# Where the rows of an elementwise multiply-and-GELU lie in DRAM: 5 KB and 64 KB rows of a partition in two stretches, or in one row of 69 KB

## The chip, the cores and the metric

The kernel runs on one core of a Trainium2 chip. The time is device microseconds (us) of that core, the median of several executions. The profile is of one execution, taken by the hardware profiler; it is told with its own span, the time from the first to the last instruction.

The core has 16 DMA engines, which move data between DRAM and the on-chip memory of 128 partitions. A transfer is issued by one instruction of a queue (here SP's and ACT's) and runs on the 16 engines as packets. VectorE (DVE) multiplies, ScalarE (ACT) computes the GELU. In this document KB is 1024 bytes, MB and GB/s are decimal as in the profile.

## What is computed

```python
# x, y: float32 of 1024 x 4096
z = x * y
out = 0.5 * z * (1 + np.tanh(np.sqrt(2 / np.pi) * (z + 0.044715 * z ** 3)))
```

Every output element depends on the elements of x and y at the same place and on nothing else. So any way of sharing the 4,194,304 elements among the 128 partitions will do, as long as x, y and out use the same one.

## The kernel before

Each partition gets 32,768 elements (128 KB) of x, y and out. They are cut into three pieces, named by their columns in the on-chip tensor `xs`: `PIECES` (line 14) has columns 0 to 1280 (5 KB of a partition), 1280 to 17664 (64 KB) and 17664 to 32768 (59 KB). x stays in `xs` whole; the product and then the GELU overwrite it in place. y goes through `ys`, which holds 20,440 elements of a partition, so the y pieces share its space (`Y_LOADS`, line 16: the columns and the place in `ys`).

`columns` (line 51) says where a piece lies in DRAM. It takes the flat tensor, picks the stretch that belongs to the piece (128 times the piece's columns, starting at 128 times its first column), and cuts this stretch into 128 rows, one for each partition. So before the change the 5 KB rows of all partitions follow each other without a gap in the first 640 KB, the 64 KB rows in the next 8 MB, and the 59 KB rows in the rest. The same function serves x, y and out.

There are nine transfers of 128 rows each, three for x, y and out. Their order:

- The 5 KB x rows (SP) and the 64 KB x rows (ACT) are issued at the very start; `_hoist` (line 25) moves the two instructions ahead of the program's opening.
- SP waits for the 5 KB x rows (line 81) and issues the 64 KB y rows, then the 59 KB x rows.
- SP issues the 59 KB y rows when three multiplications are done (their place in `ys` is then free), and the 5 KB y rows when four are (`Y_FREE`, line 18).
- VectorE multiplies the 64 KB piece in four steps of 4096 columns, the 59 KB piece in seven steps of 2048 and one of 768, and the 5 KB piece in one step (`STEPS`, line 20; line 99). ScalarE follows each step (line 107).
- SP stores in the order of `STORES` (line 21): the 64 KB rows, the 59 KB rows, the 5 KB rows. The first store waits until the 59 KB y rows have landed (line 114), and each for ScalarE (line 115).
- At the end SP waits for the stores and clears the semaphores (lines 117 to 122).

Of the kernel before, what the change touches and what calls it, by code (L numbers as in the profile page):

```python
# [1 line left out]

# [4 lines left out]


F32 = mybir.dt.float32
GELU = mybir.ActivationFunctionType.Gelu_apprx_tanh  # L10

PIECES = [(0, 1280), (1280, 17664), (17664, 32768)]

Y_LOADS = [(1280, 17664, 4056), (17664, 32768, 0), (0, 1280, 15104)]

Y_FREE = [0, 3, 4]

STEPS = [[4096] * 4, [2048] * 7 + [768], [1280]]  # L20
STORES = [(1280, 17664), (17664, 32768), (0, 1280)]
Y_BUF = 20440


def _hoist(nc, issued):

    here = nc.cur_bb.bb.instructions
    first = nc.main_func.blocks[0].instructions
    for ins in issued:
        del here[next(k for k, i in enumerate(here) if i is ins or i.name == ins.name)]  # L30
    engine = issued[0].engine
    at = next(
        k
        for k, i in enumerate(first)
        if i.engine == engine and type(i).__name__ == "InstDrain"
    )
    first[at:at] = issued


@with_exitstack  # L40
def kernel(
    ctx: ExitStack,
    tc: tile.TileContext,
    x: bass.AP,
    y: bass.AP,
    out: bass.AP,
):
    nc = tc.nc
    P = nc.NUM_PARTITIONS

    def columns(t, a, b):

        flat = t.flatten_outer_dims().rearrange("r c -> (r c)")
        pa, pb = next(q for q in PIECES if q[0] <= a and b <= q[1])
        return flat[P * pa : P * pb].rearrange("(p c) -> p c", p=P)[:, a - pa : b - pa]


    tc.close()
    tc.compile()

    xs = nc.alloc_sbuf_tensor("xs", [P, PIECES[-1][1]], F32).ap()
    ys = nc.alloc_sbuf_tensor("ys", [P, Y_BUF], F32).ap()
    sem_x = [nc.alloc_semaphore(f"sem_x{i}") for i in range(len(PIECES))]
    sem_y = [nc.alloc_semaphore(f"sem_y{i}") for i in range(len(Y_LOADS))]
    sem_mul = nc.alloc_semaphore("sem_mul")
    sem_act = nc.alloc_semaphore("sem_act")
    sem_o = [nc.alloc_semaphore(f"sem_o{i}") for i in range(len(STORES))]

    def load_x(i, engine=nc.sync):
        a, b = PIECES[i]  # L70
        return engine.dma_start(out=xs[:, a:b], in_=columns(x, a, b)).then_inc(sem_x[i], 16)

    def load_y(i):
        a, b, r = Y_LOADS[i]
        return nc.sync.dma_start(
            out=ys[:, r : r + b - a], in_=columns(y, a, b)
        ).then_inc(sem_y[i], 16)

    _hoist(nc, [load_x(0).ins])
    _hoist(nc, [load_x(1, nc.scalar).ins])  # L80
    nc.sync.wait_ge(sem_x[0], 16)
    load_y(0)
    load_x(2)
    for i in range(1, len(Y_LOADS)):
        if Y_FREE[i]:
            nc.sync.wait_ge(sem_mul, Y_FREE[i])
        load_y(i)

    nc.scalar.wait_ge(sem_x[0], 16)
    n = 0  # L90
    done = {}
    for i, (a, b, r) in enumerate(Y_LOADS):
        for j, (xa, xb) in enumerate(PIECES):
            if xa <= a < xb:
                nc.vector.wait_ge(sem_x[j], 16)
        nc.vector.wait_ge(sem_y[i], 16)  # L96
        c = a
        for w in STEPS[i]:
            nc.vector.tensor_mul(  # L99
                out=xs[:, c : c + w],  # L100
                in0=xs[:, c : c + w],
                in1=ys[:, r + c - a : r + c - a + w],
            ).then_inc(sem_mul, 1)
            n += 1
            done[c + w] = n
            nc.scalar.wait_ge(sem_mul, n)
            nc.scalar.activation(  # L107
                out=xs[:, c : c + w], in_=xs[:, c : c + w], func=GELU
            ).then_inc(sem_act, 1)
            c += w  # L110

    for i, (a, b) in enumerate(STORES):
        if i == 0:
            nc.sync.wait_ge(sem_y[-2], 16)
        nc.sync.wait_ge(sem_act, done[b])
        nc.sync.dma_start(out=columns(out, a, b), in_=xs[:, a:b]).then_inc(sem_o[i], 16)
    for i in range(len(STORES) - 1):
        nc.sync.wait_ge(sem_o[i], 16)
    nums = sorted(s.num for s in [*sem_x, *sem_y, *sem_o[:-1], sem_mul, sem_act])
    assert nums == list(range(nums[0], nums[-1] + 1))  # L120
    nc.sync.sem_clear(range(nums[0], nums[-1] + 1))
    nc.sync.wait_ge(sem_o[-1], 16).then_inc(sem_o[-1], -16)


# [1 line left out]
_INS = ['x', 'y']  # L126
_OUTS = [((1024, 4096), 'float32')]


# [23 lines left out]
```

## Time and profile before

| | |
|---|---|
| median of 3 runs | 119.72 us (119.71 to 119.9) |
| span of the profiled execution | 118.5 us |
| VectorE busy | 35.2 us in 13 instructions |
| ScalarE busy | 30.9 us in 14 instructions |
| moved by DMA | 50.33 MB: 33.55 read, 16.78 written |
| mean rate over the span | 425 GB/s |

The profiled execution's time outside its span is not in the profile; the span is 1.2 us below the median. The 50.33 MB are the two inputs and the output once each.

How the profile's DMA rows are read: each row of a transfer is one packet here. A queue's row gives the number of packets (a few tiny ones are semaphore updates), the megabytes, and the time that its packets took as a share of 16 engines' span. In a table of stretches each line has the stretch, its length, the busy time and number of instructions of VectorE, ScalarE and GpSimd, the granted TensorE clock, the DMA engines' busy share, and GB/s. A packet is counted whole where it starts, so a share can come out a little over 1 in a stretch that is cut through packets.

The transfers, from their issue to the landing of the last byte (the 64 KB ones come without their size in this view):

```profile
xs<-in_x_dram SPq DMA_DIRECT2D x1, 7552.0 KB, 46.5
ys<-in_y_dram SPq DMA_DIRECT2D x1, 7552.0 KB, 22.5
out_dram<-xs SPq DMA_DIRECT2D x1, 7552.0 KB, 20.4
xs<-in_x_dram SPq DMA_DIRECT2D x1, 640.0 KB, 13.6
ys<-in_y_dram SPq DMA_DIRECT2D x1, 640.0 KB, 19.7
out_dram<-xs SPq DMA_DIRECT2D x1, 640.0 KB, 20.8
xs<-in_x_dram ACTq DMA_DIRECT2D x1, 30.4
ys<-in_y_dram SPq DMA_DIRECT2D x1, 29.0
```

These are long because a transfer waits in its queue behind others: the 640 KB of y's 5 KB rows land 19.7 us after their issue.

### The profile page before, as it was taken

The numbers are of one execution on the slowest core, as the hardware profiler recorded it, in microseconds if no ns is written. First come the engines' busy times: TensorE is split into PE (matmuls) and PEld (weight loads), VectorE is DVE, ScalarE is ACT, GpSimd is POOL, SyncE is SP. The second block draws the span as 40 slices with busy tenths as digits, with TensorE's granted clock in tenths as the row PEclk, the third lists the DMA queues.
The fourth block names the chain that finished last, engine by engine and source line by source line (L and its number), as shares of the span: only waits on it lengthen the run. The fifth ranks groups of instructions, "written<-read, shape, count | busy, mean of one in ns | idle before, by whom it ended". The sixth has DMA issues, their size and how long they took to land.

```text
span 118.5 us, 83 instructions
## 1 busy us (share of the span) xinstructions
DVE 35.2 (30%) x13; ACT 30.9 (26%) x14; POOL 0.2 (0%) x4
## 2 busy tenths in 40 slices
DVE  0000000000000069999920000059999940000000
ACT  0000000000000000999975000006998990000000
POOL 0000000000000000000000000000000000000000
DMA  9888899889988897798797797798899887977975
GB/s 492 382 382 382 354 597 464 354 354 465 597 354 354 354 632 347 326 632 347 326 632 347 326 632 347 326 575 354 354 531 531 354 354 326 653 326 326 653 326 221
DMA packets 1296, 50.33 MB, mean 425 GB/s; under 512 B 144, under 2 KB 144, under 8 KB 528
## 3 DMA queue, kind: packets, MB, share of 16 engines
q1 hardware_dynamic: 1152, 41.94, 82.3%
q10 hardware_dynamic: 144, 8.39, 16.5%
HBM read 33.55 MB, written 16.78 MB: 425 GB/s over the span
## 4 chain that ended last, share of the span: by engine, by line
DMA 55%; DVE 24%; ACT 3%; issue 1%; DVEq 0%
DMA ys<-in_y_dram 43%; DVE xs L99 24%; DMA xs<-in_x_dram 11%; ACT xs L107 3%; DVEq L96 0%
## 5 line engine op out<-in xcount | busy, mean ns | idle before, releaser
L99 DVE TENSOR_TENSOR xs<-xs,ys 128x2048 f32<-128x2048 f32 (+3 forms) x13 | 35.2, 2778 | 60.9 <-DMA ys<-in_y_dram 60.9
L107 ACT ACTIVATE xs<-xs 128x2048 f32<-128x2048 f32 (+3 forms) x13 | 29.6, 2300 | 19.6 <-DVE xs L99 19.6
L107 ACT ACT_TABLE_LOAD x1 | 1.3, 1283 | 47.2 <-DVE xs L99 47.2
L137 POOL MEMSET const-uint8-127<- 128x1 uint8 x1 | 0.1, 102 | 0.0
L137 POOL MEMSET const-bfloat16-1.0<- 128x1 bf16 x1 | 0.1, 101 | 0.0
L137 POOL MEMSET const-float32-0.0<- 128x1 f32 x1 | 0.1, 98 | 0.2 <-issue 0.2
L137 POOL MEMSET const-float32-1.0<- 128x1 f32 x1 | 0.1, 98 | 0.0
## 6 DMA issues: line engine op xcount, KB each, us to landing
xs<-in_x_dram SPq DMA_DIRECT2D x1, 7552.0 KB, 46.5
ys<-in_y_dram SPq DMA_DIRECT2D x1, 7552.0 KB, 22.5
out_dram<-xs SPq DMA_DIRECT2D x1, 7552.0 KB, 20.4
xs<-in_x_dram SPq DMA_DIRECT2D x1, 640.0 KB, 13.6
ys<-in_y_dram SPq DMA_DIRECT2D x1, 640.0 KB, 19.7
out_dram<-xs SPq DMA_DIRECT2D x1, 640.0 KB, 20.8
xs<-in_x_dram ACTq DMA_DIRECT2D x1, 30.4
ys<-in_y_dram SPq DMA_DIRECT2D x1, 29.0
```

The source lines that it names most:

```text
L99: nc.vector.tensor_mul(out=xs[:, c : c + w], in0=xs[:, c : c + w], in1=ys[:, r + c - a : r + c - a + w],).then_inc(sem_mul, 1)
L107: nc.scalar.activation(out=xs[:, c : c + w], in_=xs[:, c : c + w], func=GELU).then_inc(sem_act, 1)
L137: nc = _bacc.Bacc("TRN2", target_bir_lowering=False, num_devices=1)
```

## The change

A second table, `STRETCHES`, has two stretches in place of the three pieces, and `columns` looks a piece up in it. The first stretch has columns 0 to 17664: in DRAM each partition has one row of 69 KB, its first 5 KB being the first piece and the other 64 KB the second. The 59 KB rows are where they were. The transfers, their order, their places on the chip, the waits and the computing are the same. The first two pieces of a partition hold other elements than before, the same ones in x, y and out.

```diff
 PIECES = [(0, 1280), (1280, 17664), (17664, 32768)]
+
+STRETCHES = [(0, 17664), (17664, 32768)]
...
         flat = t.flatten_outer_dims().rearrange("r c -> (r c)")
-        pa, pb = next(q for q in PIECES if q[0] <= a and b <= q[1])
+        pa, pb = next(q for q in STRETCHES if q[0] <= a and b <= q[1])
         return flat[P * pa : P * pb].rearrange("(p c) -> p c", p=P)[:, a - pa : b - pa]
```

| rows of x, y and out | first row at, before | pitch before | first row at, after | pitch after |
|---|---|---|---|---|
| 5 KB | 0 | 5 KB | 0 | 69 KB |
| 64 KB | 640 KB | 64 KB | 5 KB | 69 KB |
| 59 KB | 8832 KB | 59 KB | 8832 KB | 59 KB |

## The prediction

> **What bounds the kernel now.** I read the page's DMA rows first, because the engines are idle most of the span:
>
> ```profile
> span 118.5 us, 83 instructions
> DVE 35.2 (30%) x13; ACT 30.9 (26%) x14; POOL 0.2 (0%) x4
> ...
> q1 hardware_dynamic: 1152, 41.94, 82.3%
> q10 hardware_dynamic: 144, 8.39, 16.5%
> ```
>
> VectorE and ScalarE together work 66 us, the two DMA queues fill 82.3 + 16.5 = 98.8% of 16 engines' span: 0.988 x 118.5 = 117.1 us of packets on each DMA engine. The kernel is a stream of 50.33 MB, and the other 1.4 us are lead-in and tail. Then the stages, cut where the stream changes its rows (stretch, its length, busy times, clock, DMA share, GB/s):
>
> ```profile
> 1.00:12.50 11.50, 0.00 (x0) 0.00 (x0) 0.00 (x0) 1.00 1.02 422
> 12.50:41.50 29.00, 0.00 (x0) 0.00 (x0) 0.00 (x0) 1.00 1.00 434
> 41.50:77.20 35.70, 17.43 (x4) 15.64 (x5) 0.00 (x0) 1.00 1.00 433
> 77.20:79.10 1.90, 0.76 (x1) 0.00 (x0) 0.00 (x0) 1.00 0.83 342
> 79.10:98.50 19.40, 17.02 (x9) 15.26 (x9) 0.00 (x0) 1.00 1.00 433
> 98.50:116.37 17.87, 0.00 (x0) 0.00 (x0) 0.00 (x0) 1.00 1.00 433
> ```
>
> 12.5 to 41.5 reads 64 KB rows (x, y), 41.5 to 77.2 reads 59 KB rows, 79.1 to 98.5 writes 64 KB rows, the last writes 59 KB rows. All four run at 433 to 434 GB/s, whether the rows lie 64 KB or 59 KB apart and whether they are read or written. So a row costs its bytes. The third view is the trace's list of DMA packets (start, duration, bytes of each): 1152 data packets, one for each row of each of nine transfers, 384 of each size, so 24 of each size on each of 16 engines. The floor is 2418 ns for 65536 bytes, 2229 for 60416, 196 for 5120. 24 x (2.418 + 2.229 + 0.196) = 116.2 us. The packets' real mean per engine is 117.0 us. The 0.8 us of excess lie here (us per engine): first x load, 5 KB rows 0.35; x 64 KB rows beside them 0.17; 64 KB stores 0.08; the other six transfers 0.1 together. Before the first packet lie 1.0 us, behind the last one 0.4: 1.0 + 117.0 + 0.4 = 118.4 of the span's 118.5.
>
> Who issues, and with what slack, from the timeline (start, length, instruction):
>
> ```profile
> 0.00 0.38 SPq L71 DMA_DIRECT2D xs<-in_x_dram  x1
> 0.12 0.36 ACTq L71 DMA_DIRECT2D xs<-in_x_dram  x1
> ...
> 13.57 0.33 SPq L75 DMA_DIRECT2D ys<-in_y_dram  x1
> 13.96 0.43 SPq L71 DMA_DIRECT2D xs<-in_x_dram  x1
> ...
> 55.79 4.66 SPq L75 DMA_DIRECT2D ys<-in_y_dram  x2
> ...
> 78.27 19.77 SPq L116 DMA_DIRECT2D out_dram<-xs  x3
> ```
>
> Only the last row is tight. The first store is issued at 78.27 and its first packets start at 79.11 to 79.45; what fills the engines meanwhile is the load of the 5 KB y rows (8 x 0.196 = 1.57 us each), which ends at 78.94 to 79.29. The mean hole is 0.1 us. The y issue at 55.79 comes 3.6 us before the rows ahead of it run out (59.4), the y load issued at 13.57 while 64 KB x rows still run to 30.
>
> **The change, part by part.** No instruction is added or removed: the same nine transfers in the same order from the same queues, of 128 rows each. What changes is the DRAM address of six of them, x, y and out of the 5 KB rows (pitch 5 KB to 69 KB) and of the 64 KB rows (pitch 64 KB to 69 KB, first row at 5 KB in place of 640 KB). The three of 59 KB rows keep addresses, pitch and order.
>
> 1. Issue: same instructions, 0.33 to 0.43 us each, hidden behind packets in flight (the hoisted two are not, but their shape is the same). 0.
>
> 2. 64 KB rows in the stream, 24 per engine. No row of before has a 69 KB pitch, so bounds. Below: their mean over three transfers is 2429 ns against 2418, so at most 24 x 0.011 = 0.26 us to gain. Above: the dearest steady level that the trace shows for them is the start of the stores, where 16 engines begin together and the first packets mean 2450 ns; if the new pitch held all 24 rows there, 24 x (2450 - 2429) = +0.5 us. The nearest row is the 59 KB transfer: also an odd number of KB apart, also not on 64 KB boundaries, and at 2230 ns in both loads against a floor of 2229. There is an arithmetic reason to take that row: the engines work on rows four partitions apart, 4 x 59 = 236 KB before, 4 x 69 = 276 KB after, and 236 + 276 = 512 KB, so below 512 KB the new starting places are the old 59 KB ones in mirror order. I take 0.
>
> 3. 5 KB rows of y and out, 16 per engine. Neighbouring rows no longer touch. Below: they are at 196 (y) and 199 ns (out), nothing to gain. Above: the mean of the first x load, 238 ns: 8 x 42 + 8 x 39 = +0.65 us; a longer y load also fills the 0.1 us hole, so +0.55. The nearest row: in that first x load, once 64 KB packets stand between the 5 KB ones (starts 2.2 to 12 us), 54 of 57 took 206 ns or less, though each follows a packet from elsewhere. Being next to its neighbour is not what makes a 5 KB row cheap. I take 0.
>
> 4. The start. 71 of the x load's 5 KB rows begin before 2.2 us and mean 268 ns; the first 64 KB packets of the 16 engines mean 2576 (up to 2858) where later ones take 2420. That is 0.35 + 0.17 us of excess, the only place where addresses visibly could matter. Below: all of it goes, -0.5. Above: as much again, +0.5. Between bounds of one size I take the middle, 0: some of the excess may fall to the first packets at any address.
>
> 5. Compute. Stores wait for ScalarE, ScalarE for VectorE, VectorE for y; none is nearer than 1 us to the stream except the first store, which follows the landing of the 59 KB y rows, unchanged. 0. If the 5 KB y rows ended earlier the hole at 79 would grow by as much; part 3 gives no reason.
>
> Sum: 118.5 + 0 = 118.5 of the profiled span; the median is 119.72, 1.2 us more, which I keep. **119.7 us.**
>
> **Rivals.**
>
> A (slower): the 69 KB pitch keeps the engines in step on the same part of the memory. Place: all 64 KB rows, and the 5 KB rows with them. Price: part 2's +0.5 and part 3's +0.55 together, 120.8; part 2 alone, 120.2. It decides once a 64 KB row costs over 10 ns more (24 x 10 = 0.24 us, 0.2%). Against it: the 59 KB rows, and DMA share 1.00 in every stage. For it: the kernel has no slack, every nanosecond of a packet shows in the end, and what the DRAM side can bear above 434 GB/s is seen nowhere.
>
> B (slower): rows of 5 KB that don't touch cost an opening each, 39 to 42 ns: 120.3. It decides alone from 15 ns a row (16 x 15 = 0.24). For it: in the first load the early ones cost up to 756 ns. Against: the 54 of 57.
>
> C (faster): 64 KB apart is a bad distance while engines are in step, at the start and at the first store, and 69 KB spreads them. Price: 0.17 + 0.08 us for the 64 KB rows, and as much of the 0.35 as follows, so 119.1 to 119.5. For it: the first 64 KB packets' 2576 ns against 2420 later, when engines have drifted apart. Against: the start itself, whatever the addresses, may explain them, and the in-step first stores cost just 32 ns more than the floor. The Trainium skill has this as a rule (DMA: Bandwidth & Descriptors, Latency and other measured facts): large power-of-two row pitches in HBM slow a copy, and a few KiB of padding restores it. The pitch of 512 KiB is still near full speed there, and the trace agrees that 64 KB is harmless in the steady stream (434 GB/s), so by the rule too little is left to gain here.
>
> That the change does nothing on the chip (the rows are moved as the same packets) is my forecast itself.
>
> **How the numbers follow.** This kernel's three times lie within 0.2% (119.71 to 119.9), so 0.24 us is what can be told from no change. Forecast, within 119.5 to 120.0: 0.42. A: 0.20, B: 0.15, C: 0.22; 0.01 for something else that is slower. I keep the rivals this high because the price of a DRAM address is just what the trace of one layout cannot show, and 10 ns in 2418 decide. Slower 0.36, faster 0.22. The range goes from 119.2 (C with most of the start's excess) to 120.9 (A in full). The likeliest case has 119.5 to 120.0 of its own.
>
> **What would show it.** Right: the four stretches again at 433 to 434 GB/s, 64 KB packets at 2418 to 2430 ns, 5 KB ones of y and out at 196 to 200, the store's issue about 78.3. Part 2 is wrong if 64 KB packets in mid-stream mean over 2440, part 3 if the y rows' stretch near 77 to 79 gets longer, part 4 if the first 12.5 us move over 0.2 us either way. The forecast as a whole is wrong if the DMA share falls below 0.98 or its packets lengthen.

## The result and the profile after

| | median | lowest to highest | runs |
|---|---|---|---|
| before | 119.75 us | 119.67 to 119.9 | 13 |
| after | 120.04 us | 119.89 to 120.18 | 13 |

The ratio is 1.0021, with a 95% interval of 1.0014 to 1.0028: the change costs 0.25 us (0.17 to 0.34). The forecast was no change with its own range up to 120.0.

The page's DMA rows of the kernel after, with the same columns as before:

```profile
span 118.6 us, 83 instructions
DVE 35.2 (30%) x13; ACT 30.9 (26%) x14; POOL 0.2 (0%) x4
...
q1 hardware_dynamic: 1152, 41.94, 82.3%
q10 hardware_dynamic: 144, 8.39, 16.4%
```

and the four long stretches, cut where they were cut before:

```profile
12.50:41.50 29.00, 0.00 (x0) 0.00 (x0) 0.00 (x0) 1.00 1.00 434
41.50:77.20 35.70, 17.43 (x4) 15.64 (x5) 0.00 (x0) 1.00 1.00 433
79.10:98.50 19.40, 17.06 (x9) 15.26 (x9) 0.00 (x0) 1.00 1.00 433
98.50:116.37 17.87, 0.00 (x0) 0.00 (x0) 0.00 (x0) 1.00 1.00 433
```

The steady stream is what it was: 433 to 434 GB/s in all four. So the loss is not spread over the 24 moved 64 KB rows of an engine. This profiled execution took 119.89 us, the fastest of its 13, and its span is just 0.05 us longer than the one before. To see the loss, a longer execution is wanted; the repeat below (after_again) left one of 120.3 us, near the upper end of its eight (120.01 to 120.34). So it shows where time is lost, and more of it than the median loses. Here is the chain of waits of the kernel before, start, length, what:

```profile
0.00 13.56 DMA xs<-in_x_dram
...
13.57 28.99 DMA ys<-in_y_dram
...
42.66 13.11 DVE xs L99 x3
...
55.79 22.46 DMA ys<-in_y_dram
```

and of after_again, the changed kernel:

```profile
0.00 13.99 DMA xs<-in_x_dram
...
14.01 29.01 DMA ys<-in_y_dram
...
43.11 13.11 DVE xs L101 x3
...
56.24 22.46 DMA ys<-in_y_dram
```

The first link, until the 5 KB x rows have landed, grew by 0.43 us. Every later link has its old length within 0.02 us, and the span is 119.0 in place of 118.5. The whole difference is there before anything but x has been asked for. The length of the first link is a sign of it and not the price itself: in x5_gap, a kernel below that loses nothing, SP asks for y 2.4 us later than before:

```profile
15.95 0.33 SPq L79 DMA_DIRECT2D ys<-in_y_dram  x1
```

There each engine had one more 5 KB row left to take turns with 64 KB rows, and the 64 KB x rows kept it busy all the while. The first 2.5 us by stretch, before, after and after_again, say the same:

```profile
0.00:2.50 2.50, 0.00 (x0) 0.00 (x0) 0.20 (x4) 1.00 1.24 452
```

```profile
0.00:2.50 2.50, 0.00 (x0) 0.00 (x0) 0.20 (x4) 1.00 0.76 234
```

```profile
0.00:2.50 2.50, 0.00 (x0) 0.00 (x0) 0.20 (x4) 1.00 0.57 109
```

A packet is counted whole where it starts, so the fall from 452 to 234 and 109 GB/s says mostly that fewer 64 KB packets had begun by then. By the packet list, in which a packet can be counted by the part that is done, the engines had moved 0.44, 0.36 and 0.24 MB by 2.5 us. 75, 63 and 38 of the 128 5 KB x rows were done, and those begun before 2.2 us took 268, 342 and 518 ns in the mean; of the later ones the middle one takes 196.

### The profile page after: what moved, and what is told of

It is laid out like the page before. It is cut to its first block, busy times and chain, and to the rows that moved or that the text cites. A ratio compares the mean times of both kernels' runs of the same rounds, so it can differ in the third digit from the quotient of the medians.

```text
span 118.6 us, 83 instructions
## 1 busy us (share of the span) xinstructions
DVE 35.2 (30%) x13; ACT 30.9 (26%) x14; POOL 0.2 (0%) x4
## 4 chain that ended last, share of the span: by engine, by line
DMA 55%; DVE 24%; ACT 3%; issue 1%; DVEq 0%
DMA ys<-in_y_dram 43%; DVE xs L101 24%; DMA xs<-in_x_dram 11%; ACT xs L109 3%; DVEq L98 0%
## 6 DMA issues: line engine op xcount, KB each, us to landing
ys<-in_y_dram SPq DMA_DIRECT2D x1, 7552.0 KB, 22.5
```

## The experiments

Each kernel ran beside the kernel before on one chip; the chip is not the same for all of them, so across the tables the ratios compare better than the times. Ratios are to the kernel before, with 95% intervals; 0.001 is 0.12 us. "Joined" is the layout after, "split" the layout before.

### Which of x, y and out

```diff
-    def columns(t, a, b):
+    def columns(t, a, b, stretches):
...
-        pa, pb = next(q for q in PIECES if q[0] <= a and b <= q[1])
+        pa, pb = next(q for q in stretches if q[0] <= a and b <= q[1])
...
-        return engine.dma_start(out=xs[:, a:b], in_=columns(x, a, b)).then_inc(sem_x[i], 16)
+        return engine.dma_start(out=xs[:, a:b], in_=columns(x, a, b, JOINED)).then_inc(sem_x[i], 16)
```

This is x_joined, where y and out get `SPLIT`; y_joined and out_joined give `JOINED` to the other two in turn. after_again is the changed kernel as it is.

> The changed kernel once more, beside its parts. If the loss is the layout's, the ratio to the kernel before is again 1.0021 (1.001 to 1.003, about +0.25 us). If it was chance between two programs, it is 1.000 within 0.001.

> Only x is read in rows of 69 KB; y and out keep the three stretches, so x and y no longer match element by element. Theory S (the start pays: the first 5 KB x rows, 69 KB apart, take longer to arrive, as their 259 ns mean against 238 in the two profiles says): the whole loss is here, ratio 1.0015 to 1.003, and the mean of the 5 KB x rows is 250 ns or more. Theories Y and O: ratio within 0.0007 of 1.

> Only y is read in rows of 69 KB; x and out keep the three stretches, so x and y no longer match element by element. Theory Y (the 5 KB y rows are what the engines have while the first store is being issued; their start moved from 77.20 to 77.29 and the hole before the first store may have grown): the loss is here, ratio 1.001 to 1.003, with the time between the last y packet of an engine and its first store packet longer than 0.1 us. Theories S and O: ratio within 0.0007 of 1.

> Only the output is written in rows of 69 KB, so its elements of the first two pieces land in other places than the reference's. Theory O (the stores of rows that don't touch need longer until their last byte is confirmed, which lies behind the last packet): the loss is here, ratio 1.001 to 1.003, and the time from the last packet's end to the span's end is above 0.4 us. Theories S and Y: ratio within 0.0007 of 1.

| kernel | median us | ratio | interval |
|---|---|---|---|
| after_again | 120.15 | 1.0028 | 1.0018 to 1.0038 |
| x_joined | 120.22 | 1.0028 | 1.0018 to 1.0039 |
| y_joined | 119.84 | 0.9999 | 0.9990 to 1.0008 |
| out_joined | 119.83 | 1.0000 | 0.9991 to 1.0009 |

The loss is real, and all of it is x's. The mean of the 5 KB x rows in x_joined was 278 ns (240 in y_joined, 237 in out_joined). Rows of y and out, 5 KB ones among them, lie 69 KB apart for nothing. Theory S stands, Y and O fall.

### Which rows of x, and how far apart

In these kernels only one transfer's rows move. `X_STRETCHES` gives the stretch of each x piece; a wider stretch puts the rows further apart. x5_pitch69:

```diff
+X_STRETCHES = [(0, 17664), (1280, 17664), (17664, 32768)]
...
-        return engine.dma_start(out=xs[:, a:b], in_=columns(x, a, b)).then_inc(sem_x[i], 16)
+        return engine.dma_start(out=xs[:, a:b], in_=columns(x, a, b, [X_STRETCHES[i]])).then_inc(sem_x[i], 16)
```

The first entry is (0, 1536) for 6 KB, (0, 4096) for 16 KB, (0, 4352) for 17 KB, (0, 32768) for 128 KB. x64_pitch69 has (0, 1280) and (0, 17664) as its first two. x5_pitch59 reads columns 17664 to 18944 of the 59 KB rows in the first load.

> Only the 5 KB x rows are read 69 KB apart; the 64 KB x rows are read where they were, so the 5 KB pieces of x and y don't match. Theory F (the first 5 KB rows pay for lying far from each other): the loss of x_joined is all here, ratio 1.0015 to 1.0035, 5 KB x rows at 255 ns or more in the mean. Theory N (the 5 KB and the 64 KB row of a partition, read at the same time by two queues, get in each other's way where they touch): ratio within 0.0007 of 1.

> Only the 64 KB x rows are read 69 KB apart, from 5 KB on; the 5 KB x rows are read in their own stretch, so the 64 KB pieces of x and y don't match. Theory F: no loss, ratio 0.998 to 1.0007; it is below 0.9995 if the in-step 64 KB rows were helped by the new pitch (first sixteen 64 KB packets under 2500 ns in the mean, 2584 before). Theory N: no loss either, since the two rows of a partition don't touch here. A loss of 1.0015 or more would say that the 64 KB rows alone make it.

> Only the 5 KB x rows move, to 16 KB apart (2 MB in all), so the 5 KB pieces of x and y don't match. Theory F with a price that grows with the distance: between the kernel before and the one with 69 KB, ratio 1.0003 to 1.0015. Theory T (not the distance counts but that rows don't touch): as with 69 KB, 1.0015 to 1.0035. Theory N: within 0.0007 of 1.

> Only the 5 KB x rows move, to 128 KB apart (16 MB in all), so the 5 KB pieces of x and y don't match. Theory F with a growing price: more than with 69 KB, ratio 1.003 to 1.006. Theory T: the same as with 69 KB. A theory of in-step engines (16 engines start 512 KB apart and meet in the same part of the memory): far more than with 69 KB, ratio above 1.005.

> Only the 5 KB x rows move, to 17 KB apart, in place of the 16 KB that lost 0.77 us; the 5 KB pieces of x and y don't match. If 16 KB is bad because the 16 engines, four rows apart, start a power of two (64 KB) from each other, 17 KB is as good as 69 KB or better: ratio 1.000 to 1.0035. If it is bad because the rows crowd a part of the memory that the 64 KB x rows read at the same time, 17 KB is as bad: 1.005 or more.

> The first load reads 5 KB rows 59 KB apart from the part of x where the 59 KB rows lie, so no other load is near them at the start (the 5 KB piece of x is not the reference's). Theory C: these rows wait as those 69 KB apart do, and the 64 KB rows wait too (first sixteen 64 KB packets near 2584 ns again), since nothing touched their part before: ratio 1.003 to 1.006. A theory of two queues that meet in one part of the memory: ratio below 1.001.

> Only the 5 KB x rows move, to 6 KB apart, so they no longer touch but cover 768 KB in place of 640; the 5 KB pieces of x and y don't match. Theory T (rows that don't touch pay): ratio 1.0015 to 1.0035, as at 17 and 69 KB. Theory R (the size of the region that the first packets spread over): within 0.0007 of 1.

| kernel | 5 KB x rows apart | median us | ratio | interval |
|---|---|---|---|---|
| before, beside them | 5 KB | 119.78 to 119.87 | 1 | |
| x5_pitch6 | 6 KB | 120.23 | 1.0040 | 1.0022 to 1.0058 |
| x5_pitch16 | 16 KB | 120.63 | 1.0064 | 1.0052 to 1.0076 |
| x5_pitch17 | 17 KB | 120.16 | 1.0018 | 1.0010 to 1.0027 |
| x5_pitch59 | 59 KB, elsewhere | 120.00 | 1.0011 | 1.0003 to 1.0020 |
| x5_pitch69 | 69 KB | 120.34 | 1.0036 | 1.0022 to 1.0050 |
| x5_pitch128 | 128 KB | 120.04 | 1.0018 | 1.0009 to 1.0026 |
| x64_pitch69 | 5 KB (64 KB rows 69 KB apart) | 119.96 | 1.0005 | 0.9996 to 1.0014 |

The 5 KB x rows alone make the loss, with the 64 KB rows where they were; so theory N, that the two rows of one partition meet where they touch, isn't needed. Every distance but 5 KB costs, and not in order of distance: a price that grows with it (the first form of F) falls by 16 against 128 KB, and the size of the region (R) falls by 6 KB, which covers only 768 KB and loses as much as 69. Theory T (rows that don't touch pay alike) foretold at most 1.0035 and is passed by 16 KB. In-step engines at a power of two explain 16 against 17 KB, but they foretold over 1.005 for 128 KB, which has 1.0018. Theory C foretold 1.003 or more for 59 KB elsewhere, and first 64 KB packets as slow as before (2576 ns in the mean of the first sixteen); it got 1.0011 and 2420 ns: that its rows are the first to touch a part of the memory is not the reason. The distance to the 64 KB rows read beside them may be: 59 KB elsewhere has the smallest ratio. But the intervals of 17, 59 and 128 KB overlap, and its distance and place were changed together.

### The 5 KB rows, or the first rows

```diff
-    _hoist(nc, [load_x(0).ins])
-    _hoist(nc, [load_x(1, nc.scalar).ins])
+    _hoist(nc, [load_x(1).ins])
+    _hoist(nc, [load_x(0, nc.scalar).ins])
```

Now SP issues the 64 KB rows and ACT, just behind, the 5 KB rows, so idle engines read 64 KB rows first. This is done to the kernel before (swap_split), to the changed one (swap_joined), to x5_pitch69 (swap_x5) and to x64_pitch69 (swap_x64).

> The kernel before with the first two loads exchanged: SP issues the 64 KB x rows, ACT the 5 KB x rows 0.1 us later. It is the partner of swap_joined. The waits for the 5 KB x rows (of SP ahead of the y load) stay. Both theories: within 0.5% of the kernel before; lower if 64 KB rows bear the first wait better, since an engine then waits with fewer packets.

> The changed kernel with the same exchange. Theory C (the first packets of the stream wait for the part of the memory that they are the first to touch; 5 KB rows spread over 8.6 MB touch more of it at once than 5 KB rows in 640 KB): the 64 KB rows now come first in both layouts, and the pair differs by less than 0.1 us. Theory F (5 KB rows that lie apart pay wherever they stand in the first load): the pair differs by 0.25 us or more, as the two kernels without the exchange do.

> The exchange of the first two loads (64 KB x rows first), and only the 5 KB x rows 69 KB apart; their elements don't match y's. Its partner is swap_split, at 1.024 of the kernel before. Theory C (the first rows that idle engines read pay, and the 5 KB rows are not first here): 1.023 to 1.0255. Theory F (5 KB rows that lie apart pay wherever they stand in the first load): 1.0265 or more.

> The exchange of the first two loads, and only the 64 KB x rows 69 KB apart; their elements don't match y's. Its partner is swap_split, at 1.024. Theory C, if 64 KB rows pay for the wider distance when they come first: 1.026 to 1.0295, the 0.4 us between swap_split and swap_joined. Theory F: 1.023 to 1.0255.

| kernel | median us | ratio | interval |
|---|---|---|---|
| swap_split | 122.76 | 1.0240 | 1.0226 to 1.0254 |
| swap_x5 | 122.79 | 1.0248 | 1.0234 to 1.0262 |
| swap_x64 | 123.13 | 1.0278 | 1.0262 to 1.0294 |
| swap_joined | 123.19 | 1.0293 | 1.0275 to 1.0312 |

All four lose 2.4% or more, which was not foreseen (0.5% was). In swap_split the two queues' packets alternate, one 5 KB row and one 64 KB row, so the last 5 KB rows land late, and SP, which waits for them, asks for y at 23.51 in place of 13.57:

```profile
0.00 0.38 SPq L71 DMA_DIRECT2D xs<-in_x_dram  x1
23.51 0.33 SPq L75 DMA_DIRECT2D ys<-in_y_dram  x1
```

By the packet list the engines end their 64 KB x rows at 22.5 and begin y's at 24.7 in the mean. That hole is common to the four; the question is what differs. Theory C had said that swap_joined and swap_split would differ by less than 0.1 us. They differ by 0.4 (123.19 against 122.76), which is what F foretold, so C as it was first put is wrong. The two kernels that move one transfer alone tell which rows do it. The 5 KB rows 69 KB apart cost nothing here (swap_x5), and in its packet list they take 196 ns each. The 64 KB rows 69 KB apart cost 0.4 us (swap_x64), though in x64_pitch69, where they came second, 0.06 us with an interval around nothing. In swap_x64's profile SP's wait ends 0.6 us later than in swap_split:

```profile
24.12 0.33 SPq L77 DMA_DIRECT2D ys<-in_y_dram  x1
```

So it is not the size of the rows that pays but their being first. That half of theory C holds, and F falls, though the pair had spoken for it.

### The form of the transfer, or the place of the rows

With 5 KB rows 5 KB apart, or 64 KB rows 64 KB apart, the DRAM side is one unbroken stretch. x5_gap and swap_x64_gap break it without moving a row; x5_gap:

```diff
+    sem_fill = nc.alloc_semaphore("sem_fill")
+    nc.gpsimd.memset(xs[:, 1264:1280], 0.0).then_inc(sem_fill, 1)
+    nc.vector.wait_ge(sem_fill, 1)
...
         a, b = PIECES[i]
+        b -= 16 * (i == 0)
```

> The kernel before, but each 5 KB x row is read 64 bytes short, at its old place; the last 16 columns of the 5 KB piece are filled with zeros by GpSimd in their stead, so those outputs are 0. Theory G (a transfer whose DRAM side is one unbroken stretch is taken apart in another way than one of separate rows, and that shows while the engines are idle): the loss is here too, ratio 1.0015 to 1.004. Theory M (the place of the rows in the memory decides): within 0.0007 of 1, since rows and places are the same.

> The kernel with the first two loads exchanged (swap_split, 1.024 of the kernel before), but each 64 KB x row is read 64 bytes short, at its old place; the last 16 columns of that piece are filled with zeros by GpSimd, so those outputs are 0. Theory G: as swap_x64, 1.026 to 1.0295. Theory M: as swap_split, 1.023 to 1.0255.

x5_gap: 119.87 us, ratio 1.0002 (0.9993 to 1.0012). swap_x64_gap: 122.64 us, 1.0236 (1.0222 to 1.0250), as swap_split. A break of 64 bytes between rows costs nothing, so theory G falls, and theory T with it, taken at its word: the addresses decide, not the form of the transfer nor that the rows touch to the byte.

### Once the first rows touch, may the others lie anywhere

```diff
+STRETCHES = [(0, 1280), (1280, 32768)]
...
-        pa, pb = next(q for q in PIECES if q[0] <= a and b <= q[1])
+        pa, pb = next(q for q in STRETCHES if q[0] <= a and b <= q[1])
```

> The 5 KB rows keep a stretch of their own, and each partition's 64 KB and 59 KB rows lie together as one row of 123 KB in x, y and out. Theories C, F and T: no loss, since the first rows touch: ratio 0.9985 to 1.0007, below 0.9995 only if the 64 KB rows that begin beside the 5 KB ones gain from the new distance. If any wide distance of rows read in the first microseconds costs: 1.0015 or more.

119.83 us, ratio 1.0008 (0.9998 to 1.0019). With the 5 KB rows in their own stretch, 64 and 59 KB rows 123 KB apart in x, y and out cost 0.1 us, with an interval that reaches nothing; and they gain nothing. No version beat the kernel before.

### How a late start reaches the end

The stream is long, and an engine that starts late could be made up for by others that run ahead. It is not, and the SP queue's rows show where it is fixed. The issue of the stores before, in after_again, x_joined, x5_pitch16 and tail_joined:

```profile
78.27 19.77 SPq L116 DMA_DIRECT2D out_dram<-xs  x3
```

```profile
78.72 19.77 SPq L118 DMA_DIRECT2D out_dram<-xs  x3
```

```profile
78.53 19.78 SPq L119 DMA_DIRECT2D out_dram<-xs  x3
```

```profile
79.12 19.78 SPq L118 DMA_DIRECT2D out_dram<-xs  x3
```

```profile
78.28 19.78 SPq L118 DMA_DIRECT2D out_dram<-xs  x3
```

Against the first, 0.45, 0.26, 0.85 and 0.01 us later; the spans are 0.45, 0.26, 0.85 and 0.02 us longer. The first store waits for the last 59 KB y row on whichever engine has it. In the packet list, the engine that comes last begins its 59 KB x rows at 42.23, 42.63, 42.45, 43.07 and 42.21 in these five, and span less that moment is 76.28 to 76.34. In the four kernels with exchanged loads it is 76.27 to 76.30, and in all twenty profiles of this document 76.27 to 76.39. The sixteenth engine's delay, not the mean, comes out at the end, one for one.

A late engine is not a thing of the changed layout alone. y_joined reads x as the kernel before does and loses nothing in the median, but its profiled execution took 120.1 us, the longest of its eleven: there the last engine begins at 42.44, and the span is 118.8. So a single execution cannot tell the layouts apart; the medians can.

## Why the prediction was wrong

*What bounds the kernel.* Right: 98.7% DMA again, and what moves the end is the stream. (The list of its excess adds up to 0.70 of the 0.8 us; the rest are the tiny semaphore packets.)

*Part 1, issue, and part 2, 64 KB rows in the stream.* Right: 2419 ns in the mean for y's rows and 2427 for out's in the profile after, 2419 and 2428 before.

*Part 3, 5 KB rows of y and out.* Right: 197 and 199 ns, and y_joined and out_joined at 0.9999 and 1.0000. The reading behind it, that 5 KB rows between other packets cost 196 ns wherever they come from, is what the runs bear out.

*Part 4, the start.* This is the step that failed. It named the place ("the only place where addresses visibly could matter"), bounded it at 0.5 us either way, and took 0, the middle "between bounds of one size", with no row that spoke for 0. The runs put +0.25 us there (0.17 to 0.34; with the repeat up to 0.46). The prediction's own sign, a move of over 0.2 us in the first 12.5, is met by after_again, whose first link grew by 0.43, and not by the profile after, where it grew by 0.03. Two readings were missed. The start held the one transfer whose rows were taken apart while the engines had nothing else, and the evidence used for part 3, rows among 64 KB packets, says nothing of that state. And the excess was counted as a mean over engines: it is 0.51 us (0.34 + 0.17) before and 0.55 after, or 0.81 in after_again, while the end follows the last engine alone.

*Part 5, compute, and the hole at 79.* Right that nothing there is late by itself. (The last engine ends the 5 KB y rows at 79.44 and not at 79.29; the mean hole is still 0.1 us.) But the first store, called the one tight place, is what turns one engine's late start into everybody's.

*The rivals.* A and B fell: they priced the steady stream and the later 5 KB rows. No rival had a loss at the start. C had the right place and the wrong sign. What it hoped for seems to come true: the first 64 KB packets fell from 2576 to 2459 ns in the mean (2433 in after_again), while the 5 KB rows ahead of them lost more. But its reason is not borne out. With the 64 KB rows alone 69 KB apart (x64_pitch69) the first 64 KB packets mean 2636 ns; with the 5 KB rows alone moved (x5_pitch69) they mean 2435. So the fall came with the 5 KB rows' new place and not with the 64 KB rows' new distance. The first 64 KB packets then also start further apart, over 0.7 us in x5_pitch69 and 0.4 before; that this is why they are faster is not shown. The Trainium skill's advice for pitches (DMA: Bandwidth & Descriptors, Latency and other measured facts), a few KiB of padding against large powers of two, has its figures for 512 KiB and more. At the smaller distances of these runs both outcomes are seen: swap_x64, with 64 KB rows first at 69 KB, is 0.4 us slower than swap_split, at 64 KB, while 5 KB rows at 17 KB lose less than at 16.

*What stays open.* Why these addresses: 5 KB apart (touching, or 64 bytes short of it) is good, 6 to 128 KB is not, 16 KB has the largest loss, and 64 KB rows read first do better 64 KB than 69 KB apart. The traces have no row for what a packet waits for inside the memory. x5_pitch6 is the hardest case: in its profile the 5 KB rows' mean is low (231 ns), and the loss is one late engine (59 KB rows from 42.57). Whether nearness to the 64 KB rows read at the same time plays a part was not tried apart from distance.

## What to carry to other kernels

In a kernel that only streams, look at the first two microseconds apart from the rest: what idle engines read first was sensitive to where its rows lie in DRAM, and the same rows later were not. Pack the first transfer's rows one behind the other in DRAM, and measure a layout there rather than infer it from the steady stream. Where a wait asks for the last engine's last packet, reckon with the latest engine, not with the mean.

## What was not expected of the hardware

- Packets of two queues alternated one row to one row, whatever their size: in swap_split 5 KB and 64 KB packets took turns on an engine, so the 640 KB that were issued 0.1 us after the 8 MB had landed only at 23.5 us, and the kernel lost 2.4%. In the kernel before, ACT's 64 KB rows begin 1.2 us after SP's 5 KB rows do, and the 5 KB rows land at 13.56.
- A distance of 16 KB between the first rows cost 0.77 us and one of 17 KB 0.2 us; with 16 KB the 64 KB x rows, which were not moved, took 2455 ns in the mean, against 2421 with 69 KB.
